# Layer 1 of a two-layer backbone: another order for its last two tiles, its weights' places and its mask's load

## The chip, the cores and the metric

One core of one Trainium2 chip runs the whole program. The time is that of one execution on the device in microseconds (us), the median of several runs. Beside it there is one execution taken by the hardware profiler, with its trace. Engines: PE is TensorE (matrix products and transposes), ACT is ScalarE, DVE is VectorE, POOL is GpSimd, SP is SyncE, which here only issues transfers. Each engine works through its instructions in order; a queue name with a q (SPq, POOLq) is an engine's sequencer when it issues a transfer.

## The reference

Two layers over 2048 latent tokens of width 1024 and 256 context tokens. Layer 0 (even) mixes latent attention and gated linear attention. Layer 1 (odd) is a neighbourhood attention over a grid of 32 by 64 tokens, with 16 heads of 64:

```python
q, k, v, z = jnp.split(h @ w_in, 4, axis=-1)          # 1024 columns each
q, k = rms_norm(heads(q), q_gain), rms_norm(heads(k), k_gain)
s = q . k (8 x 16 neighbours) * 64 ** -0.5 + bias     # and q . k_ctx * 64 ** -0.5
o = softmax(s) @ [v of the neighbours, v_ctx]
x = x + gate * ((o * silu(z)) @ w_out)
```

The products are kept in fp32 precision.

## The kernel before

**Products.** A matrix is split into a part hi that TensorE's fast fp32 format holds and the rest lo; a product is three matmuls, hi by hi (line 129), hi by lo (130) and lo by hi (131), over 8 slices of 128 rows: 24 matmuls of 128 x 512 for one cell. A cell is a tile t of 128 tokens (18 of them, 0 and 1 being context) by a group j of 512 columns of layer 1's weight `w_od`: j=0,1 are queries, 2,3 keys, 4,5 values, 6,7 the gate z.

**Weights.** Each j has 8 slices of 256 KB. A slice is loaded by SP into one of three buffers `wraw` (line 380), ACT copies it to the hi part (the helper at line 106), DVE subtracts for the lo part (line 383). The 32 KB a partition of one j, hi and lo, lies in one of four places, w0 to w3, and `OD_PLACE` says which. Places 0 and 1 belong to one pool, 2 and 3 to another. A generator, `od_steps`, makes the steps of one weight; `pump` takes a step at every fourth call while cells run, so that loads and splits are spread among them.

**Stages of layer 1.** `even_mix` ends layer 0 and loads j=2,3 ahead. `odd_qk` (line 1144) runs the cells of j=2,3,0,1 tile by tile, loads j=0,1 at the start and, each time the last cell of a j is done, loads one of the other four weights into the place that came free (`nxt`, `done`). Its last two tiles are written out by hand: all of j=0, then 1, 2, 3, and then j=6 on the same two tiles:

```python
cells += [(t, j) for j in (0, 1, 2, 3, 6) for t in (NT - 2, NT - 1)]
```

So from the second of these ten cells on, of some 5.5 us each, the 32 slices of the last four weights pass through `wraw`.

After a cell of `odd_qk` an activation squares it, DVE sums (`oss`) and scales it (`onat`, line 1182), and five steps into a later cell `fin` transposes it (`tp`, line 1190), scales it (`oqh`) and stores it: queries to `Q1` (hi and lo) and keys to `K1` from SP, keys besides as hi and lo in another layout, gathered over four tiles (`okt`), to `K1t` from POOL (`store_k`, line 1227, four stores of 512 KB for a block of four tiles). For j=6 the stores are z's, from POOL (line 1194).

`odd_vz` (line 1257) then runs j=7,4,5 for tiles 17 and 16, after that j=4 to 7 for the other tiles downwards, and at the very end j=4,5 alone for the context tiles 1 and 0. Woven in are the row maxima of the scores (`maxes`), which read back `K1` (`mk`), `Q1` (`mq`) and a table (`mtab`).

`odd_attention` (line 1356) works on eight pairs of heads. It loads the pair's keys of the context (`kc`), chunks of keys (`kt`), queries (`q`, hi and lo in `q10`, `q11` and `q20`, `q21`), values (`ov`) and two tables of biases (`tab0`, `tab1`, 517 KB each), all on SP and in the order written, since `load` chains them. POOL adds the mask `maskk` to both tables in place (line 1420). PE makes the scores (`st`, lines 1423 and 1424), DVE adds the table (`opt`, line 1587), ACT takes the exponential. For the first pair the loads are written ahead of the loop, the mask's last:

```python
Q[0, 1] = query(0, 1)
kt.append(chunk(0, 0))
V[0] = values(0)
tabs[0] = tables(0)
kc[0] = keys(0, 0, CTX, kcp, "kc")
Q[0, 0] = query(0, 0)
kt.append(chunk(0, 1))
values_ctx(0, V[0])
mk = self.tl(ap, [P, NR, NC], "maskk", bufs=1)
self.load(mk[:], self.i["maskk"].rearrange("p (r c) -> p r c", r=NR))
mask(tabs[0])
```

Buffers of the stages share the on-chip memory: a tile of a later stage lies where tiles of an earlier one were, and its load waits for their last reader. Waits and places follow from the pools; the order in which each engine gets its instructions is worked out when the program is built.

Of the kernel before, what the change touches and what calls it, by code (L numbers as in the profile page):

```python
# [10 lines left out]
F32 = mybir.dt.float32  # L11
F32R = mybir.dt.float32r
AF = mybir.ActivationFunctionType
ALU = mybir.AluOpType
# [3 lines left out]
P = 128  # L18
# [3 lines left out]
CTX = 256  # L22
# [66 lines left out]
class Kern:  # L89
# [919 lines left out]
    def even_mix(self, e1, win, hT):  # L1009
# [3 lines left out]
        with ExitStack() as es:  # L1013
# [57 lines left out]
            self.prep_pool(e1, "prp1", "left", 2, 3)  # L1071
            ws = [self.pool(e1, "owS", side="left", reuse_waits="tile")]

            def ahead():
                for j in (2, 3):
                    yield from self.od_steps(win, j, ws)
                for t in range(2):
                    hT[t] = self.prep(1, t, self.x1, pp, ("pj", 4))
                    yield
                    yield  # L1080
# [51 lines left out]
            next(ahead, None)  # L1132


    OD_PLACE = {2: 0, 3: 1, 0: 2, 1: 3, 4: 0, 5: 1, 6: 2, 7: 3}

    def od_steps(self, dst, j, ws):
        n = self.OD_PLACE[j]
        steps = self.split_steps(dst, j, ws[n // 2], self.i["w_od"][:, j], KD, 512, f"w{n}", 1)
        for k, _ in enumerate(steps):  # L1140
            if k % 2:
                yield

    def odd_qk(self, ws, win, hT):
        nc = self.nc
        self.V1c = self.scr("V1c", (2, P, NCT, 512), F32)
        self.V1 = self.scr("V1", (2, SEQ, 512), F32)
        self.Q1 = self.scr("Q1", (2, 8, P, SEQ), F32)
        self.z1 = self.scr("z1", (KD, P, SEQ), F32)
        self.K1 = self.scr("K1", (8, P, T), F32)  # L1150
        self.K1t = self.scr("K1t", (8, 2, P, T), F32)
        with ExitStack() as es:
            sp = self.pool(es, "osA", bufs=2, side="left", reuse_waits="tile")
            pp = self.pool(es, "opA", bufs=2, space=PSUM, reuse_waits="tile")
            qkg = self.tl(sp, [P, 2], "oqkg", bufs=1)
            nc.sync.dma_start(qkg[:], self.i["od_gain"])
            nc.vector.tensor_scalar(out=qkg[:, 0:1], in0=qkg[:, 0:1], scalar1=0.125, scalar2=None, op0=ALU.mult)
            self.ahead += [self.od_steps(win, 0, ws), self.od_steps(win, 1, ws)]
            pend, kt = [], {}

            def cell(t, j):
                hi, lo = hT[t]
                wh, wl = win[j]
                ps = self.tl(pp, [P, 8, 64], "gm", bufs=3)
                steps = self.mm3_steps(ps[:], (lambda k: hi[:, k, :], lambda k: lo[:, k, :]),
                                       (lambda k: wh[:, k, :], lambda k: wl[:, k, :]), range(KD))
                for n, _ in enumerate(steps):
                    if n == 5 and pend and (len(pend) > 1 or j == 6):
                        fin(*pend.pop(0))
                    yield  # L1170
                if j == 6:
                    n = self.tl(sp, [P, 512], "onat", bufs=4)
                    self.gate(n, ps[:].rearrange("p h d -> p (h d)"))
                    pend.append((t, j, n))
                    return
                sq = self.tl(sp, [P, 512], "osq")
                self.act(sq[:], ps[:].rearrange("p h d -> p (h d)"), AF.Square)
                ss = self.tl(sp, [P, 8], "oss", bufs=4)
                nc.vector.tensor_reduce(out=ss[:], in_=sq[:].rearrange("p (h d) -> p h d", h=8), axis=AX.X, op=ALU.add)
                self.rpow(ss[:], ss[:], 1.0 / 64, EPS)  # L1180
                n = self.tl(sp, [P, 512], "onat", bufs=4)
                nc.vector.tensor_tensor(out=n[:].rearrange("p (h d) -> p h d", h=8), in0=ps[:],
                                        in1=ss[:].unsqueeze(2).to_broadcast([P, 8, 64]), op=ALU.mult)
                pend.append((t, j, n))

            def fin(t, j, n):
                z = j // 2
                ps = self.tl(pp, [P, 4, P], "tp")
                for i in range(4):
                    nc.tensor.transpose(ps[:, i, :], n[:, i * P : i * P + P], self.ident[:])  # L1190
                hi = self.tl(sp, [P, 4, P], "oqh", F32R)
                if j == 6:
                    self.act(hi[:].bitcast(F32), ps[:])
                    nc.gpsimd.dma_start(self.z1[:4, :, (t - NCT) * P : (t - NCT) * P + P].rearrange("j p t -> p j t"), hi[:].bitcast(F32))
                    return
                self.act(hi[:], ps[:], AF.Copy, scale=qkg[:, z : z + 1])
                j0 = (j % 2) * 4
                if z == 1:
                    nc.sync.dma_start(self.K1[j0 : j0 + 4, :, t * P : t * P + P].rearrange("j p t -> p j t"), hi[:].bitcast(F32))
                if z == 0 or t < NCT:  # L1200
                    lo = self.tl(sp, [P, 4, P], "oql", F32R)
                    nc.vector.scalar_tensor_tensor(out=lo[:], in0=ps[:], scalar=qkg[:, z : z + 1], in1=hi[:],
                                                   op0=ALU.mult, op1=ALU.subtract)
                    if z == 0:
                        for part, tt in enumerate((hi, lo)):
                            nc.sync.dma_start(self.Q1[part][j0 : j0 + 4, :, (t - NCT) * P : (t - NCT) * P + P].rearrange("j p t -> p j t"),
                                              tt[:].bitcast(F32))
                    else:
                        store_k((hi, lo), j0, t * P, P)
                    return  # L1210
                g, r0 = divmod(2 * (t - NCT), 8)
                if r0 == 0:
                    kt[j] = [self.tl(sp, [P, 4, 512], f"okt{j}{part}", F32R, bufs=1) for part in range(2)]
                view = lambda x, n: x[:].rearrange("p i (r c b) -> p i r c b", r=n, c=4)
                for r in range(2):
                    oh, ol = (x[:].rearrange("p i (c b r) -> p i r c b", c=4, r=8)[:, :, r0 + r] for x in kt[j])
                    self.act(oh, view(ps, 2)[:, :, r], AF.Copy, scale=qkg[:, z : z + 1])
                    nc.vector.scalar_tensor_tensor(out=ol, in0=view(ps, 2)[:, :, r], scalar=qkg[:, z : z + 1],
                                                   in1=view(hi, 2)[:, :, r], op0=ALU.mult, op1=ALU.subtract)
                if r0 == 6:  # L1220
                    store_k(kt.pop(j), j0, CTX + g * 512, 512)

            def store_k(parts, j0, o, w):

                for u, x in enumerate(parts):
                    for i in range(2):
                        nc.gpsimd.dma_start(self.K1t[j0 : j0 + 4, i, u * 64 : u * 64 + 64, o : o + w].rearrange("j d t -> d j t"),
                                            x[i * 64 : i * 64 + 64].bitcast(F32))

            nxt = {2: 4, 3: 5, 0: 6, 1: 7}  # L1230
            done = lambda j: j in nxt and self.ahead.append(self.od_steps(win, nxt[j], ws))
            cells = self.cells(list(range(NT)), (2, 3, 0, 1), lambda t, j: j > 1 or t >= NCT)[:-8]
            cells += [(t, j) for j in (0, 1, 2, 3, 6) for t in (NT - 2, NT - 1)]
            for _ in self.stream(cells, hT, cell, lambda t: self.prep(1, t, self.x1, pp, ("px", 2)), done):
                self.pump()
            while pend:
                fin(*pend.pop(0))

    def gate(self, out, in_):

# [115 lines left out]
    def odd_attention(self, out, right, left, wout):  # L1356
# [4 lines left out]
        with ExitStack() as es:  # L1361
# [53 lines left out]
                    self.load(tb[:], self.i["rpb_k"][2 * j + i].rearrange("p (r c) -> p r c", r=NR))  # L1415
                return tabs

            def mask(tabs):
                for tb in tabs:
                    nc.gpsimd.tensor_tensor(out=tb[:], in0=tb[:], in1=mk[:], op=ALU.add)  # L1420

            def scores(ps, k1, k2, q1, q2):
                nc.tensor.matmul(ps, k1, q1, start=True, stop=False)  # L1423
# [87 lines left out]
            kt.append(chunk(0, 0))  # L1511
            V[0] = values(0)
            tabs[0] = tables(0)
            kc[0] = keys(0, 0, CTX, kcp, "kc")
            Q[0, 0] = query(0, 0)
            kt.append(chunk(0, 1))
            values_ctx(0, V[0])
            mk = self.tl(ap, [P, NR, NC], "maskk", bufs=1)
            self.load(mk[:], self.i["maskk"].rearrange("p (r c) -> p r c", r=NR))
            mask(tabs[0])  # L1520
            out_w, out_s = weights(), split()
            pend, late, OA = [], [], {}
            all_k, most_k = slice(0, KD), slice(0, KD - 1)
# [18 lines left out]
            for j in range(8):  # L1542
                OA[j] = {}, {}
                for s, (kind, n) in enumerate(steps):
                    g, c = divmod(n, 4)
                    if j < 7:
# [10 lines left out]
                            kc[j + 1] = keys(j + 1, 0, CTX, kcp, "kc")  # L1557
                        elif s == 10:
                            with self.tc.issue_after(self.psum.ins):
                                mask(tabs[j + 1])  # L1560
                    elif s % 2 and s < 16:
                        next(out_w)
                    pts = exps() if kind == "l" else [exps(), exps()]
# [197 lines left out]
```

## Time and profile before

| what | value |
|---|---|
| median of 3 runs | 3673.76 us (3667.17 to 3674.72) |
| profiled execution | 3676.2 us, span 3674.1 us |
| granted TensorE clock, mean | 0.982 |
| loads of `w_od` slices | 64 of 256 KB |
| key stores `K1t` | 32 of 512 KB, from POOL |

In the trace, times run from the start of the span. `odd_qk` starts at 2172 us, the ten cells of its last two tiles at 2547, `odd_vz` at 2623 (its first cell), the attention at 3088.9. A group reads: line, engine, operation, result<-operands. A wait reads: who waited at which line, for whom; total us, times, longest. A DMA's time in the chain runs from its issue to its landing. The clock column is the share of full TensorE speed that was granted, 0.5 being half speed.

### The profile page before, as it was taken

What the parts mean: (1) busy time and instruction counts of PE and PEld (TensorE: products, weight loads), DVE (VectorE), ACT (ScalarE), POOL (GpSimd) and SP (SyncE); (2) the same over time, 40 slices, a digit from 0 to 9 for tenths busy, and PEclk for the clock granted to TensorE, in tenths of its full rate; (3) what the DMA queues carried; (4) which work ended last, traced back from release to release, by engine and by line L of the source; (5) the groups of instructions that cost most, each with busy time, mean ns of one, the idle gap of its engine ahead of it and who ended that gap; (6) DMA issues with size and microseconds to landing.
All of it is one profiled execution on the core that took longest, in us unless ns stands there. A gap on an engine that the chain in (4) does not pass through costs nothing.

```text
span 3674.1 us, 51831 instructions
## 1 busy us (share of the span) xinstructions
PE 3565.7 (97%) x18404; PEld 2758.7 (75%) x18404; DVE 2363.0 (64%) x4860; ACT 1437.0 (39%) x2741; POOL 1205.6 (33%) x1336
## 2 busy tenths in 40 slices
PE   8999999999999999999999999999899999999998
PEld 6988998888886666655556878888688887555577
DVE  4677666888876666687664444454578784666721
ACT  5545551111125555555553124444422223555510
POOL 1433330101111212122201233333334443777743
PEclk9999999999999999999999999999999999999899
DMA  7455472222241232243622544455744447788554
GB/s 253 145 155 155 133 210 87 80 73 88 75 137 53 83 98 79 85 115 109 177 67 96 188 161 123 141 157 160 227 146 122 146 120 190 210 215 219 175 178 149
DMA packets 364372, 512.19 MB, mean 139 GB/s; under 512 B 25825, under 2 KB 243889, under 8 KB 358210
## 3 DMA queue, kind: packets, MB, share of 16 engines
q1 hardware_dynamic: 322642, 425.49, 39.8%
q0 software_dynamic: 19872, 55.92, 5.1%
q10 hardware_dynamic: 21600, 27.46, 2.1%
q8 instruction: 146, 2.39, 0.3%
q14 instruction: 112, 0.92, 0.1%
HBM read 329.38 MB, written 179.37 MB: 138 GB/s over the span
## 4 chain that ended last, share of the span: by engine, by line
PE 69%; issue 15%; POOL 5%; DVE 5%; DMA 4%; ACT 2%; SPq 0%; POOLq 0%; DVEq 0%; ACTq 0%
PE av L922 7%; PE gm L129 6%; PE gm L130 6%; PE gm L131 6%; PE st L980 4%; PE st L981 4%; PE st L982 4%; PE st L129 2%; PE st L131 2%; PE st L130 2%; PE pj L131 2%; PE pj L130 2%; PE pj L129 2%; PE o L1456 2%; DMA wraw<-w_od 1%
## 5 line engine op out<-in xcount | busy, mean ns | idle before, releaser
L971 DVE TENSOR_TENSOR acc<-acc,apt 128x512 f32<-128x512 f32 x512 | 364.8, 737 | 153.5 <-ACT apt L106 150.6
L106 ACT ACTIVATE apt<-st 128x512 f32<-128x512 f32 (+1 forms) x592 | 344.6, 594 | 290.5 <-PE st L982 257.4
L662 DVE TENSOR_REDUCE mm<-mx 128x1 f32<-128x512 f32 (+1 forms) x656 | 393.2, 630 | 89.9 <-PE mx L661 81.8
L922 PE MATMUL av<-apt,av 128*64 128x512 f32 (+1 forms) x1184 | 286.4, 599 | 0.0
L980 PE MATMUL st<-aq,akh 97*128 97x512 f32 (+1 forms) x592 | 255.7, 432 | 9.7 <-DMA aq<-QT 6.1
L661 PE MATMUL mx<-mk,mq 96*128 96x512 f32 (+1 forms) x656 | 238.6, 372 | 0.0
L981 PE MATMUL st<-aq,akh 96*128 96x512 f32 (+1 forms) x592 | 236.7, 400 | 0.0
L982 PE MATMUL st<-aq,akl 96*128 96x512 f32 (+1 forms) x592 | 235.3, 398 | 0.0
L1330 DVE CUSTOM_DVE_ANT_1 mx<-mx,mtab 128x217 f32<-128x217 f32 (+11 forms) x576 | 184.6, 338 | 49.2 <-PE mx L1324 37.9
L106 ACT ACTIVATE opt<-opt 128x930 f32<-128x930 f32 (+9 forms) x144 | 119.2, 830 | 248.0 <-POOL opt L1627 141.0
L106 ACT ACTIVATE u<-gm 128x352 f32<-128x352 f32 (+1 forms) x144 | 70.5, 496 | 360.4 <-PE gm L131 208.7
L1587 DVE TENSOR_TENSOR opt<-st,tab 128x64 f32<-128x64 f32 (+10 forms) x576 | 142.8, 316 | 88.2 <-PE st L1424 58.1
L922 PEld LDWEIGHTS av<-apt,av 128*64 128x64 f32 x1184 | 81.9, 138 | 156.4 <-issue 154.8
L980 PEld LDWEIGHTS st<-aq,akh 97*128 97x128 f32 x592 | 113.5, 192 | 101.6 <-issue 49.5
L1462 POOL TENSOR_TENSOR oacc<-oacc,opt 128x682 f32<-128x682 f32 (+10 forms) x144 | 169.8, 1199 | 26.4 <-ACT opt L106 25.1
L982 PEld LDWEIGHTS st<-aq,akl 96*128 96x128 f32 x592 | 114.6, 194 | 25.8
L661 PEld LDWEIGHTS mx<-mk,mq 96*128 96x128 f32 x656 | 122.7, 188 | 11.7
L981 PEld LDWEIGHTS st<-aq,akh 96*128 96x128 f32 x592 | 115.3, 195 | 18.3
L1423 PE MATMUL st<-q,kt 128*128 128x480 f32 (+5 forms) x256 | 99.6, 391 | 23.8 <-DVE opt L1587 18.9
L106 ACT ACTIVATE x<-px,modB,modA 128x128 f32<-128x128 f32 x272 | 99.3, 469 | 58.1 <-PE px L331 46.3
L129 PE MATMUL gm<-w0h,hhi 128*128 128x512 f32 x288 | 116.1, 403 | 0.0
L129 PE MATMUL gm<-w1h,hhi 128*128 128x512 f32 x288 | 115.7, 402 | 0.0
(570 smaller groups left out, 9928.1 us busy)
## 6 DMA issues: line engine op xcount, KB each, us to landing
q<-Q SPq DMA_DIRECT2D x48, 512.0 KB
H<-x ACTq DMA_DIRECT2D x36, 512.0 KB
adaw<-ada_w SPq DMA_DIRECT2D x64, 256.0 KB
x<-H SPq DMA_DIRECT2D x32, 512.0 KB
wraw<-w_od SPq DMA_DIRECT2D x64, 256.0 KB
K1t<-okt POOLq DMA_DIRECT2D x32, 512.0 KB, 7.6
kt<-K1t SPq DMA_DIRECT2D x32, 512.0 KB
mtab<-rpb_q SPq DMA_DIRECT2D x16, 899.0 KB
```

The lines of the kernel that those rows point to most:

```text
L106: return self.nc.scalar.activation(out, in_, func, **kw)
L129: self.nc.tensor.matmul(out, lh(k), rh(k), start=j == 0, stop=False)
L130: self.nc.tensor.matmul(out, lh(k), rl(k), start=False, stop=False)
L131: yield self.nc.tensor.matmul(out, ll(k), rh(k), start=False, stop=j == n - 1)
L661: mm = nc.tensor.matmul(ps[:, :w], q[:A_QK, (t % 6) * P : (t % 6) * P + P], k[:A_QK, k0 : k0 + w], start=True, stop=True)
L662: nc.vector.tensor_reduce(out=m[:, t, n : n + 1], in_=ps[:, :w], axis=AX.X, op=ALU.max)
L922: nc.tensor.matmul(O[j, nb][i * 64 : i * 64 + 64, :w], V[j, kt // TT][:, kt % TT, i * 64 : i * 64 + 64], pts[i][:, :w], start=n == 0, stop ...
L971: nc.vector.tensor_tensor(out=acc[i][:, :w], in0=a[:, :w], in1=pts[i][:, :w], op=ALU.add)
L980: nc.tensor.matmul(ps[:, :w], kh[: A_QK + 1, i, kq], qh[: A_QK + 1, :w], start=True, stop=False)
L981: nc.tensor.matmul(ps[:, :w], kh[:A_QK, i, kq], ql[:A_QK, :w], start=False, stop=False)
L982: mm = nc.tensor.matmul(ps[:, :w], kl[:A_QK, i, kq], qh[:A_QK, :w], start=False, stop=True)
L1330: nc.vector.tensor_tensor_reduce(out=s, in0=s, in1=tb[:, ri : ri + rn, ci : ci + cn], scale=1.0, scalar=-3e38, op0=ALU.add, op1=ALU.max, a ...
```

## The change

One generator now makes the steps for all weights in a list `todo`, two slices at a step, and splits the slices of the step before while it loads two new ones. `od_ahead` adds weights to the list:

```diff
-    OD_PLACE = {2: 0, 3: 1, 0: 2, 1: 3, 4: 0, 5: 1, 6: 2, 7: 3}
-
-    def od_steps(self, dst, j, ws):
-        n = self.OD_PLACE[j]
-        steps = self.split_steps(dst, j, ws[n // 2], self.i["w_od"][:, j], KD, 512, f"w{n}", 1)
-        for k, _ in enumerate(steps):
-            if k % 2:
-                yield
+    OD_PLACE = {2: 0, 3: 1, 0: 2, 1: 3, 6: 0, 7: 1, 4: 2, 5: 3}
+
+    def od_steps(self, dst, ws):
+
+        nc, todo, old, k = self.nc, self.todo, [], KD
+        while True:
+            new = []
+            for i in range(2):
+                if i < len(old):
+                    w, hi, lo = old[i]
+                    self.act(hi, w[:])
+                    nc.vector.tensor_tensor(out=lo, in0=w[:], in1=hi, op=ALU.subtract)
+                if k == KD and todo:
+                    j, k = todo.pop(0), 0
+                    n = self.OD_PLACE[j]
+                    dst[j] = [self.tl(ws[n // 2], [P, KD, 512], f"w{n}" + z, F32R, bufs=1) for z in "hl"]
+                if k < KD:
+                    w = self.tl(self.prp, [P, 512], "wraw", bufs=self.wbufs)
+                    nc.sync.dma_start(w[:], self.i["w_od"][:, j, k])
+                    new.append((w, *(x[:, k, :] for x in dst[j])))
+                    k += 1
+            old = new
+            if not (old or todo):
+                return
+            yield
+
+    def od_ahead(self, dst, ws, *js):
+
+        self.todo += js
+        if not self.ahead:
+            self.ahead.append(self.od_steps(dst, ws))
```

The key stores of a block are handed out one at a time, at every fourth step of a later cell; the last two tiles take j=2,3, then 0,1, then 6; the gate's weights 6 and 7 follow the keys and the values' 4 and 5 the queries, in other places than before:

```diff
+                    if n % 4 == 1 and out_k:
+                        out_k.pop(0)()
                     yield
...
                 if r0 == 6:
-                    store_k(kt.pop(j), j0, CTX + g * 512, 512)
+                    out_k.extend(store_k(kt.pop(j), j0, CTX + g * 512, 512))
...
-            nxt = {2: 4, 3: 5, 0: 6, 1: 7}
-            done = lambda j: j in nxt and self.ahead.append(self.od_steps(win, nxt[j], ws))
+            nxt = {2: 6, 3: 7, 0: 4, 1: 5}
+            done = lambda j: j in nxt and self.od_ahead(win, ws, nxt[j])
...
-            cells += [(t, j) for j in (0, 1, 2, 3, 6) for t in (NT - 2, NT - 1)]
+            cells += [(t, j) for j in (2, 3, 0, 1, 6) for t in (NT - 2, NT - 1)]
```

In the attention the first pair's tables take the mask from a copy of its own, loaded right behind them into a query buffer; the lasting copy is loaded where it was:

```diff
             tabs[0] = tables(0)
+            first = self.tl(qa, [P, SEQ], "q10", bufs=2)[:, : NR * NC]
+            mask(tabs[0], load_mask(first.rearrange("p (r c) -> p r c", r=NR)))
             kc[0] = keys(0, 0, CTX, kcp, "kc")
...
-            mk = self.tl(ap, [P, NR, NC], "maskk", bufs=1)
-            self.load(mk[:], self.i["maskk"].rearrange("p (r c) -> p r c", r=NR))
-            mask(tabs[0])
+            mk = load_mask(self.tl(ap, [P, NR, NC], "maskk", bufs=1)[:])
```

More of the change, by code (lines that the diff above doesn't have):

```diff
@@ L1072, in even_mix @@
             ws = [self.pool(e1, "owS", side="left", reuse_waits="tile")]
+            self.todo = [2, 3]
             def ahead():
-                for j in (2, 3):
-                    yield from self.od_steps(win, j, ws)
+                yield from self.od_steps(win, ws)
                 for t in range(2):
@@ L1157, in odd_qk @@
             nc.vector.tensor_scalar(out=qkg[:, 0:1], in0=qkg[:, 0:1], scalar1=0.125, scalar2=None, op0=ALU.mult)
-            self.ahead += [self.od_steps(win, 0, ws), self.od_steps(win, 1, ws)]
-            pend, kt = [], {}
+            self.od_ahead(win, ws, 0, 1)
+            pend, kt, out_k = [], {}, []
             def cell(t, j):
@@ L1208, in fin @@
                     else:
-                        store_k((hi, lo), j0, t * P, P)
+                        for f in store_k((hi, lo), j0, t * P, P):
+                            f()
                     return
@@ L1220, in fin, with store @@
                 if r0 == 6:
-                    store_k(kt.pop(j), j0, CTX + g * 512, 512)
+                    out_k.extend(store_k(kt.pop(j), j0, CTX + g * 512, 512))
             def store_k(parts, j0, o, w):
[L1225 to L1228, printed above, removed]
-            nxt = {2: 4, 3: 5, 0: 6, 1: 7}
-            done = lambda j: j in nxt and self.ahead.append(self.od_steps(win, nxt[j], ws))
+                def store(u, x, i):
+                    nc.gpsimd.dma_start(self.K1t[j0 : j0 + 4, i, u * 64 : u * 64 + 64, o : o + w].rearrange("j d t -> d j t"),
+                                        x[i * 64 : i * 64 + 64].bitcast(F32))
+                return [lambda u=u, x=x, i=i: store(u, x, i) for u, x in enumerate(parts) for i in range(2)]
+            nxt = {2: 6, 3: 7, 0: 4, 1: 5}
+            done = lambda j: j in nxt and self.od_ahead(win, ws, nxt[j])
             cells = self.cells(list(range(NT)), (2, 3, 0, 1), lambda t, j: j > 1 or t >= NCT)[:-8]
-            cells += [(t, j) for j in (0, 1, 2, 3, 6) for t in (NT - 2, NT - 1)]
+            cells += [(t, j) for j in (2, 3, 0, 1, 6) for t in (NT - 2, NT - 1)]
             for _ in self.stream(cells, hT, cell, lambda t: self.prep(1, t, self.x1, pp, ("px", 2)), done):
@@ L1237, in odd_qk @@
                 fin(*pend.pop(0))
+            for f in out_k:
+                f()
     def gate(self, out, in_):
@@ L1416, in tables, with mask, load_mask @@
                 return tabs
-            def mask(tabs):
+            def mask(tabs, mk):
                 for tb in tabs:
-                    nc.gpsimd.tensor_tensor(out=tb[:], in0=tb[:], in1=mk[:], op=ALU.add)
+                    nc.gpsimd.tensor_tensor(out=tb[:], in0=tb[:], in1=mk, op=ALU.add)
+            def load_mask(mk):
+                self.load(mk, self.i["maskk"].rearrange("p (r c) -> p r c", r=NR))
+                return mk
             def scores(ps, k1, k2, q1, q2):
@@ L1559, in odd_attention @@
                             with self.tc.issue_after(self.psum.ins):
-                                mask(tabs[j + 1])
+                                mask(tabs[j + 1], mk)
                     elif s % 2 and s < 16:
```

## The prediction

> **What bounds the kernel now.** I read the engines' shares first, then a table of windows over layer 1, then what TensorE (PE) waited for there, and last the chain that ended last.
>
> ```profile
> span 3674.1 us, 51831 instructions
> PE 3565.7 (97%) x18404; PEld 2758.7 (75%) x18404; DVE 2363.0 (64%) x4860; ACT 1437.0 (39%) x2741; POOL 1205.6 (33%) x1336
> ```
>
> PE is busy for 97% of the span, and the change takes no matmul away and adds none. So only PE's idle time and its time at a low clock can be won or lost. In the stretch that the change touches (windows; the columns are length, PE, PEld, DVE, ACT, POOL, then granted clock, DMA share, GB/s):
>
> ```profile
> 2570.00:2600.00 30.00, 30.00 (x142) 24.71 (x142) 20.71 (x33) 15.97 (x28) 10.94 (x11) 1.00 0.82 245
> 2600.00:2645.00 45.00, 31.16 (x124) 24.28 (x123) 17.73 (x31) 18.41 (x31) 12.26 (x14) 0.81 0.87 279
> ```
>
> The first row, the middle of the last two tiles, runs 142 matmuls in 30 us with no gap; the second, their end, only 124 in 45 us. At 4.73 per us, 124 need 26 us, so some 18 us are lost. What PE waited for between 2150 and 2700 (total, times, longest):
>
> ```profile
> PE tp L1190 <- DVE onat L1182: 8.4, 3, 6.7
> PE tp L1282 <- DVE ovz L1242: 3.1, 1, 3.1
> PE tp L1190 <- ACT oqh L106: 3.0, 1, 3.0
> PE px L331 <- DVE x L328: 2.9, 1, 2.9
> ```
>
> The last row stands at the start of the stage (2195 us); the others are the tail. Their 6.7 + 3.1 + 3.0, the 0.8 us of a short one, and two stretches at half clock make the 18 us. Behind them, by the chain of waits, stand transfers, not engines:
>
> ```profile
> 2605.32 2.80 DMA wraw<-w_od
> ...
> 2611.56 8.38 DMA wraw<-w_od
> ...
> 2626.11 10.73 DMA z<-oqh
> ```
>
> A 256 KB weight slice that takes 2.80 us at 2605 takes 8.38 us at 2611. In between POOL issues the first burst of key stores; a second one goes out just ahead of the gate's store (POOL's timeline):
>
> ```profile
> 2605.99 1.31 POOL L1227 DMA_DIRECT2D K1t<-okt  x2 [6.67 <-ACT okt L106]
> ...
> 2623.64 2.48 POOL L1227 DMA_DIRECT2D K1t<-okt  x4 [0.33 <-ACT okt L106]
> 2626.11 0.76 POOL L1194 DMA_DIRECT2D z<-oqh  x1
> ```
>
> DVE works in order. The split of the late slice (2614.88, after 4.15 us of idling) stands before the gate's normalising step, and with that the 6.7 us stall of PE ends:
>
> ```profile
> 2614.88 0.69 DVE L383 TENSOR_TENSOR w1l<-wraw,w1h 128x512 fp32r<-128x512 f32 x1 [4.15 <-ACT w1h L106]
> ```
>
> **The change part by part.** The order of the instructions on each engine, as the two programs are built, is the same up to the last two tiles, names apart; SP and POOL first differ at about 2570 us. The load-ahead written as one generator, and the key stores handed out singly, hence move nothing before that point: 0 us, and the 2.9 us wait at 2195 stays. Even the single stores still come out four in a row for a block of keys. No work has to hide these edits, since no instruction changes its place; if one did, the nearest price is that wait, 2.9 us either way.
>
> *The tail.* The transfers that meet there (count, KB, median us to landing):
>
> ```profile
> wraw<-w_od SPq DMA_DIRECT2D x29, 256.0 KB
> K1t<-okt POOLq DMA_DIRECT2D x8, 512.0 KB, 7.9
> ...
> Q<-oqh SPq DMA_DIRECT2D x4, 256.0 KB
> Q<-oql SPq DMA_DIRECT2D x4, 256.0 KB
> K<-oqh SPq DMA_DIRECT2D x4, 256.0 KB
> ...
> z<-oqh POOLq DMA_DIRECT2D x2, 256.0 KB, 9.0
> ...
> V<-ovz POOLq DMA_DIRECT2D x4, 128.0 KB, 2.4
> ```
>
> Bytes are not saved, only reordered. With keys first the two bursts (8 x 512 KB = 4.2 MB) go out with the fourth and the sixth cell, at about 2578 and 2593 instead of 2606 and 2624, in the middle of the 32 slices. In the built program 25 slices are split before the gate's second activation, against 29 now. Now, what has landed by then is 29 slices, half the key stores, and the Q and K stores: 7.6 + 2.1 + 3.1 = 12.8 MB in the 44 us from 2570 to 2614, 290 GB/s. Afterwards it is 25 slices, all key stores and the K stores, 6.6 + 4.2 + 1.0 = 11.8 MB: 41 us at that rate, 48 us at the 245 GB/s of the first row. So the gate is freed between 2610.7 and 2618.2; I take 2614.1, between the two, since the bursts sit where the 245 was measured with no burst in it. The gate's transposes and the next cell follow 3.5 us later when no late slice stands between them (a normalising step, an activation, a DVE step and three transpose groups of 0.4 to 0.7 us), so that cell starts at 2617.6. Now it starts at
>
> ```profile
> 2623.03 0.78 PE L129 MATMUL gm<-w3h,hhi 128*128 128x512 f32 x1
> ```
>
> which is a gain of 5.4 us (1.3 to 8.8). The gate's store has no burst ahead of it any more: instead of 10.73 us it takes some 3 us, near the 2.4 us of the V stores on the same queue. Then DVE's memsets do not hold up ovz, and the 3.1 us of PE go, with 1.6 us of the half clock after it. Against that, the loads of the maxima (keys, table, queries) stand behind the last slice on SP: I allow 1.3 us (0 to 3), about one slice's share of the stream. Tail: -(5.4 + 3.1 + 1.6 - 1.3) = **-8.8 us**, with ends of -2 and -14.
>
> By the Trainium skill ("Trainium Kernel Development and Optimization", Key Constraints) transfers issued from SP, ACT and POOL all run on the same 16 DMA engines and interleave. That speaks against this part, since bursts on POOL take from the slices on SP wherever they are put. The 8.38 us against 2.80 us agree with it; by it alone the tail would gain nothing, which is the first rival below.
>
> *The places of the weights.* This part is in the dictionary alone, and the change does not tell of it. Weights j=4 and 5 (the values) move from places 0 and 1 to places 2 and 3. The attention's first keys, tables and queries lie in the memory of places 2 and 3, as the built programs show. The last four cells of the values stage are tiles 1 and 0 with j=4 and 5. Today they use places 0 and 1, so the loads below go out 20 to 28 us before these cells end (SP's timeline; the last row is the mask, which waits for the last cell):
>
> ```profile
> 3060.54 1.08 SPq L111 DMA_DIRECT2D kt<-K1t  x2
> ...
> 3065.81 1.45 SPq L111 DMA_DIRECT2D tab<-rpb_k  x2
> ...
> 3068.43 2.60 SPq L111 DMA_DIRECT2D q<-Q  x3
> ...
> 3088.69 0.34 SPq L111 DMA_DIRECT2D maskk<-maskk  x1
> ```
>
> ```profile
> SPq L111 <- PE gm L131: 13.1, 3, 7.0
> ```
>
> That SP waits for matmuls of the projection here shows this reuse. Afterwards the first table has to wait for the low part of the very last cell, as the mask does now: 3088.69. SP is in order, so behind it queue the second table, the mask's copy, the first head's context keys and its queries, and PE's first score needs those queries. Sizes:
>
> ```profile
> q<-Q SPq DMA_DIRECT2D x6, 512.0 KB
> tab<-rpb_k SPq DMA_DIRECT2D x3, 517.0 KB
> ...
> maskk<-maskk SPq DMA_DIRECT2D x1, 517.0 KB
> ...
> kc<-K1t SPq DMA_DIRECT2D x1, 256.0 KB
> kc<-K1t SPq DMA_DIRECT2D x1, 128.0 KB
> ```
>
> 517 x 3 + 384 + 512 x 2 = 2959 KB. The first 517 KB take the time of the mask today,
>
> ```profile
> 3088.69 5.56 DMA maskk<-maskk
> ```
>
> and the other 2442 KB (2.50 MB) a rate that I take from windows around this place:
>
> ```profile
> 3070.00:3084.00 14.00, 14.00 (x65) 11.52 (x64) 0.00 (x0) 1.20 (x2) 1.18 (x2) 1.00 1.05 277
> ...
> 3088.00:3101.20 13.20, 8.96 (x36) 6.76 (x35) 7.90 (x20) 5.41 (x11) 5.37 (x4) 0.86 0.85 202
> 3101.20:3106.40 5.20, 5.20 (x18) 1.49 (x17) 1.20 (x9) 1.88 (x3) 4.96 (x4) 0.70 0.98 332
> ```
>
> The 277 GB/s hold for just these transfers: 9.0 us. The ends are 332 (7.5) and 216 of its slowest 4 us (11.6), the 202 being lowered by waits. So PE stalls 5.56 + 9.0 - 0.1 = 14.5 us (13.0 to 17.1). What stands there today goes,
>
> ```profile
> PE st L1423 <- DVE opt L1587: 4.2, 2, 3.6
> ```
>
> because the copy of the mask lands three transfers before the queries and POOL's two additions run meanwhile. The half clock that follows today, (1 - 0.86) x 13.2 + (1 - 0.70) x 5.2 = 3.4 us, stays, as a longer stall will not shorten it. All that waits behind the queries on SP (the next keys, the context values, the mask itself, the second head's queries) is late too; for that I add 1.5 us (0 to 4). Start of the attention: 14.5 - 4.2 + 1.5 = **+11.8 us** (8 to 17).
>
> By the Trainium skill ("DMA: Bandwidth & Descriptors", Where 436 GB/s comes from) a transfer between HBM and SBUF is bound by the HBM's share of one core, about 358 GB/s. By it the 2.50 MB would take 7.0 us and this part come to +9.8; no row here reaches that, so the sum goes by 277.
>
> *Sum:* -8.8 + 11.8 = +3.0 us. The profiled execution took 3676.2 us, 2.1 more than its span, so it would become 3679.2. It lies 2.4 us above the median of the runs; from 3673.76 I reach **3677 us**.
>
> **The rivals.** *The tail gains nothing* (slower): the bursts slow the slices in the middle as much as they do now at the end, the gate waits until 2618 or beyond, and the store of z and the loads of the maxima make a new wait. For it speaks the DMA share of 0.82 in the 30 us in which the bursts will come; against it, that today's slices wait only in the 8 us after a burst. Then -2 in the tail and +11.8 at the attention: 3684, up to 3689. It decides if a slice takes over 7 us at both bursts.
>
> *The loads are quick and the tail clears* (faster): of the 18 us all but 4 go, and the attention's loads run at 332 GB/s without a late effect: -14 + 8 = -6, 3668; with the half clock also cut, 3665. For it speaks that the tail's stalls all hang on transfers that move away; against it, that both ends must come together.
>
> *The mask alone* (faster): the attention's loads do not wait for the last cells, and the change does what its words say: 4.2 + 3.4 go at the attention and 8.8 in the tail, 3657. The reuse of places 2 and 3 speaks against it.
>
> **How the numbers follow.** Forecast 0.50, no gain in the tail 0.38, quick loads 0.09 (3662 to 3671), the mask alone 0.03. A measurement of this kernel can tell about 0.2% (7.3 us) from no change: faster is below 3666.4, slower above 3681.1. The forecast's own range, 3669 to 3685, lies mostly between; about a quarter of it is slower (0.12), and of the first rival some five sixths (0.32). Faster takes the mask alone (0.03), half of the quick loads (0.05) and the lowest end of the forecast (0.02). That gives 0.10 faster, 0.46 within, 0.44 slower. The range with 8 of 10 goes from 3667 to 3690: it leaves out the mask alone, half of the quick loads, and the worst end of the first rival.
>
> **What would show it.** Right: a gap of PE of 13 to 17 us before the first st of the attention, ended by a DMA of q; a wait of SP on gm just before the tables; no wait of st for opt of 3 us; the K1t stores in the tail some 28 us earlier; 7.5 us from the last product ahead of the gate's transposes to the next cell, where there are 12.9 now (to 2623.03), and no wait for ovz. Wrong: 11 us or more there, or the wait for ovz kept (the first rival), or table loads issued before the last cells end (the third), or a difference ahead of the last two tiles, which I hold to be nought.

## The result, and the profile after

| | before | after |
|---|---|---|
| median | 3673.76 us (3667.17 to 3675.64, 9 runs) | 3681.65 us (3677.87 to 3687.29, 9 runs) |
| ratio, 95% interval | | 1.0030 (1.0022 to 1.0039) |
| profiled execution, span | 3676.2, 3674.1 us | 3686.8, 3685.0 us |

The change makes the kernel slower, by 0.3% as the ratio has it (the two medians lie 7.9 us apart). The interval lies clear of no change. The time is 4.6 us above the predicted 3677, inside the range.

Four places of PE's timeline split the 10.9 us between the two spans: the first product of the stage of queries and keys (2172.03 us before, 2174.83 after), the end of the last product of the values stage (3088.89, 3090.52), the first score of the second pair of heads (3134.72, 3150.49), and the end of the span.

| stretch | before | after | difference |
|---|---|---|---|
| up to layer 1's first product | 2172.0 | 2174.8 | +2.8 |
| the two projection stages | 916.9 | 915.7 | -1.2 |
| attention, up to the second pair of heads | 45.8 | 60.0 | +14.1 |
| the rest of attention, and output | 539.4 | 534.5 | -4.9 |

The first row lies ahead of the first instruction that differs: two executions of one program differ by as much. The second and third are the prediction's two terms. In the last row the profile of before is the odd one: all other profiles of this document, of either order, have 532.2 to 537.0 us there.

The windows of the changed kernel's end of `odd_qk`, and of the attention's start (columns as before, the last three being clock, DMA share and GB/s):

```profile
2570.00:2600.00 30.00, 30.00 (x143) 24.75 (x142) 19.57 (x32) 19.04 (x34) 12.09 (x14) 1.00 0.71 219
2600.00:2645.00 45.00, 34.09 (x144) 27.07 (x142) 21.19 (x36) 17.11 (x30) 10.33 (x12) 0.85 0.88 270
...
3088.00:3118.00 30.00, 15.60 (x45) 11.35 (x46) 8.28 (x24) 6.81 (x12) 7.38 (x6) 0.63 0.95 241
```

In the last row PE works half of 30 us, at a granted clock of 0.63. For the first pair of heads, from its first score to the second pair's, the gap of PE left out, the clock was lower than before:

```profile
3104.52:3150.50 45.98, 44.87 (x261) 29.67 (x261) 23.42 (x71) 21.13 (x33) 27.80 (x23) 0.84 0.84 211
```

against 0.93 over the 45.8 us of before (3088.89 to 3134.71).

What PE waited for, at the tail (2150 to 2700 us), in the changed kernel:

```profile
PE tp L1216 <- DVE onat L1273: 8.2, 2, 6.8
PE px L331 <- DVE x L328: 4.5, 1, 4.5
PE tp L1216 <- DVE onat L1208: 2.2, 1, 2.2
...
PE mx L1348 <- ACT mz L106: 0.9, 1, 0.9
```

and at the attention's start (3060 to 3135 us):

```profile
PE st L1458 <- DMA q<-Q: 14.0, 1, 14.0
```

The wait for ovz (3.1 us) is gone, and so is the wait of the scores for the masked table (4.2 us). The wait for the gate is not: 8.2 us in place of 6.7 and 3.0. And one of 14.0 us stands where PE ran on before. SP's timeline of the changed kernel tells its cause:

```profile
3079.56 1.07 SPq L111 DMA_DIRECT2D kt<-K1t  x2
3080.86 0.41 SPq L111 DMA_DIRECT2D ov<-V  x1
3090.31 0.83 SPq L111 DMA_DIRECT2D tab<-rpb_k  x2
3091.19 0.42 SPq L111 DMA_DIRECT2D q<-maskk  x1
3091.71 1.01 SPq L111 DMA_DIRECT2D kc<-K1t  x2
3092.82 2.06 SPq L111 DMA_DIRECT2D q<-Q  x3
```

The tables, issued at 3065.81 before, go out at 3090.31, 0.2 us ahead of the end of the last projection product; mask, context keys and queries follow in line. The last of the queries that PE needs, in the chain of waits:

```profile
3093.46 10.93 DMA q<-Q
```

The bursts of key stores did move, some 23 to 25 us earlier (POOL's timeline, changed kernel). The store of z now has none close ahead of it:

```profile
2583.04 1.31 POOL L1254 DMA_DIRECT2D K1t<-okt  x2
2585.31 1.24 POOL L1254 DMA_DIRECT2D K1t<-okt  x2 [0.96 <-DVE onat L1208]
...
2598.81 1.30 POOL L1254 DMA_DIRECT2D K1t<-okt  x2 [9.46 <-ACT okt L106]
...
2600.50 1.25 POOL L1254 DMA_DIRECT2D K1t<-okt  x2
...
2626.91 0.83 POOL L1220 DMA_DIRECT2D z<-oqh  x1 [15.27 <-ACT oqh L106]
```

but the slice issued behind each burst is as late as the one of before was (8.38 us), against 2.5 us for a slice on its own (chain of waits, changed kernel):

```profile
2586.38 8.71 DMA wraw<-w_od
...
2604.51 10.67 DMA wraw<-w_od
...
2622.72 2.48 DMA wraw<-w_od
```

### The profile page after: what moved, and what is told of

Read it like the earlier page. It is cut to its first block, busy times and chain, and to the rows that moved or that the text cites. A ratio compares the mean times of both kernels' runs of the same rounds, so it can differ in the third digit from the quotient of the medians.

```text
span 3685.0 us, 51822 instructions
## 1 busy us (share of the span) xinstructions
PE 3565.4 (97%) x18404; PEld 2758.8 (75%) x18404; DVE 2363.8 (64%) x4860; ACT 1438.1 (39%) x2741; POOL 1206.1 (33%) x1336
## 4 chain that ended last, share of the span: by engine, by line
PE 68%; issue 15%; DVE 5%; DMA 5%; POOL 4%; ACT 3%; SPq 0%; POOLq 0%; DVEq 0%; ACTq 0%
PE av L922 7%; PE gm L129 6%; PE gm L131 6%; PE gm L130 6%; PE st L980 4%; PE st L981 3%; PE st L982 3%; PE o L1491 2%; PE st L129 2%; PE st L131 2%; PE st L130 2%; PE st L1458 2%; PE pj L131 2%; PE pj L130 2%; PE pj L129 2%
## 5 line engine op out<-in xcount | busy, mean ns | idle before, releaser
L1497 POOL TENSOR_TENSOR oacc<-oacc,opt 128x682 f32<-128x682 f32 (+9 forms) x144 | 169.6, 1202 | 18.7 <-ACT opt L106 17.3
L202 POOL TENSOR_TENSOR oss<-oss,mhalf 128x8 f32<-128x8 f32 x68 | 112.8, 1659 | 5.1
```

## The experiments

### The places of the values' weights

First, the context tiles moved in the values stage, so that the last four cells read places 0 and 1:

```diff
             cells = [(t, j) for j in (7, 4, 5) for t in (NT - 1, NT - 2)]
-            cells += self.cells(list(range(NT))[::-1], (4, 5, 6, 7), lambda t, j: j < 6 or t >= NCT)[8:]
+            cells += [(t, j) for j in (4, 5) for t in (1, 0)]
+            cells += self.cells(list(range(NCT, NT))[::-1], (4, 5, 6, 7))[8:]
```

> The changed kernel, and in the values stage the context tiles 1 and 0 go right after tiles 17 and 16, so that the last four cells are those of the gate (j=6,7) in places 0 and 1, and places 2 and 3 fall free four cells (some 22 us) earlier. Theory (the attention's first loads wait for the last reader of places 2 and 3): the 14.0 us gap ahead of the first score falls under 1 us and with it the half clock behind it (some 3 to 4 us); about 3682 - 17 = 3665 us. Rival (the mask's copy, 517 KB more ahead of the queries on SP, makes the stall): a gap of 10 us or more stays and the time stays within 5 us of 3682.

Measured: 3683.86 us, ratio to before 1.0025 (1.0014 to 1.0036). The wait for q is gone: the tables go out at 3061.88. But the time is not better, as another wait stands there (PE's waits at the attention's start, and the chain behind them):

```profile
PE tp L1313 <- ACT ozt L106: 12.9, 2, 10.3
```

```profile
3087.53 10.20 DMA z<-ozt
...
3098.45 2.16 DMA z<-ozt
```

The last four cells are now the gate's. Each puts its transposed result into the one buffer `ozt` and stores it. One such store of 256 KB queues behind the attention's loads and takes 10.20 us; the next, when these are through, 2.16. So the theory's place was right and its price went elsewhere. Next, therefore, the same with the gate written back into its own tile, which leaves four tiles to take turns:

```diff
-                n = self.tl(sp, [P, 512], "ovz", bufs=3)
+                n = self.tl(sp, [P, 512], "ovz", bufs=4)
...
-                z = self.tl(sp, [P, 4, P], "ozt", bufs=1)
-                self.act(z[:], pt[:])
+                z = n[:].rearrange("p (i t) -> p i t", i=4)
+                self.act(z, pt[:])
```

> The changed kernel with the context tiles early in the values stage, and the transposed gate written back into its own tile, of which there are four, in place of one separate buffer. Theory (with the context early, what was left was PE waiting 10.3 us for that one buffer, whose store queued behind the attention's loads): no wait over 2 us between the last cells and the scores, and as the tail of the odd_qk stage is some 3 us shorter, 3665 to 3670 us, faster than both. Rival (the transfers at that place are too many in any order): a wait of 8 us or more turns up at another buffer or at the first scores, 3678 to 3684 us.

Measured: 3669.06 us, ratio to before 0.9991 (0.9982 to 1.0000). Left at that place are these waits:

```profile
PE st L1459 <- DVE opt L1623: 2.3, 4, 1.1
PE tp L1313 <- ACT ovz L106: 2.2, 1, 2.2
```

The second is slightly over the 2 us expected. The stall is gone with its cause. "Faster than both" is not clear of noise against the kernel of before, as the interval ends at 1.0000. As a control, the gate in place alone, on the changed kernel:

> The changed kernel with the transposed gate written back into its own tile alone, the context tiles last. Theory (the places of the values' weights make the stall): the gap of 13 to 15 us ahead of the first score stays, 3679 to 3683 us. Rival (the one buffer of the transposed gate slowed the whole stage): the time falls by more than 5 us with the gap still there.

Measured: 3682.24 us (ratio to before 1.0023, 1.0014 to 1.0031), with

```profile
PE st L1458 <- DMA q<-Q: 13.8, 1, 13.8
```

So the 13 us between these last two kernels are the place of the last cells' weights, not the buffer. The stretch from the last projection product to the second pair of heads says the same: 46.5 us with the context early, 58.7 without.

### The mask's copy

The changed kernel without the copy (the mask loaded last, as before):

> The changed kernel without the mask's copy: the mask is loaded last, as before. Theory (places): 517 KB less stand ahead of the queries, so PE waits some 12 us for q instead of 14.0, and then 2 to 5 us for the masked table, whose load now stands behind queries and keys; 3681 to 3685 us. Rival (the copy makes the stall): no gap over 3 us ahead of the first score, the old one of 4.2 us at the table, 3671 to 3674 us.

Measured: 3684.03 us, ratio to before 1.0029 (1.0019 to 1.0038).

```profile
PE st L1454 <- DMA q<-Q: 12.4, 1, 12.4
PE st L1454 <- DVE opt L1618: 1.7, 2, 1.1
```

The stall is there without the copy. With 517 KB (0.53 MB) less ahead of the queries it is 1.6 us shorter: 331 GB/s for what is added to such a queue, by two single executions. The table's wait of 1.7 us is below the 2 to 5 expected; the scores on context keys cover most of it. And the other way round, the copy alone on the kernel of before:

> The kernel of before with the mask's copy alone. Theory (the places decide, and in the old places the copy lands early): the 4.2 us that the scores wait for the masked table go, and the half clock behind them (3.4 us), with no wait for queries in their place; about 3674 - 7 = 3667 us. Rival (the copy delays the queries): PE waits for q at the first score by 2 us or more, and the time is 3674 or above.

Measured: 3672.72 us, ratio 0.9993 (0.9985 to 1.0002). The same stretch (3080 to 3130 us) with the copy and, for comparison, in the next kernel, which has the program of before:

```profile
PE st L1427 <- DVE opt L1591: 2.1, 3, 1.1
```

```profile
PE st L1454 <- DVE opt L1618: 3.4, 2, 2.3
```

The copy shortens the wait, with no wait for queries in its place; so the rival misses too. But it is worth 1 to 2 us, not 7: in that execution of the old order the wait is 3.4 instead of 4.2, and 2.1 of it stay with the copy. From the last projection product to the second pair of heads it takes 42.7 us, against 45.1 to 45.8 in three profiles of the old order without the copy; then the second pair takes 47.4 us instead of 46.0, so about half is given back. A gain of 7 us is outside the interval, 2 inside. What it is worth in the time is not resolved here.

### The load-ahead and the single stores

> The load-ahead as one generator and the key stores handed out singly, with the old order of the last two tiles, the old places and the old mask. Each engine has the same instructions in the same order as before. Theory: no difference, 3674 us within 2 us, and the wait at 2195 us between 2.5 and 4.5 us as executions differ. Rival (these two parts cost the 1 to 2 us by which that wait was longer after): 3676 us, the wait at 4.5.

Measured: 3672.85 us (3663.28 to 3679.0), ratio 0.9993 (0.9983 to 1.0003); the wait at 2195 us was 2.6. The two parts do nothing that these runs can tell, as expected; the 4.5 us of the changed kernel's profile is a matter of one execution (2.3 to 3.3 in five other profiles of that order).

### The tail

The eight key stores of the last block held back on POOL, behind the second store of z (`zstore`), on the changed kernel:

```diff
-                    if n % 4 == 1 and out_k:
+                    if n % 4 == 1 and out_k and t < NT - 2:
...
+            with self.tc.issue_after(self.zstore.ins):
                 for f in out_k:
                     f()
```

> The changed kernel with the eight key stores of the last block held back on POOL behind the second store of z, so that no burst runs beside the 32 weight slices. Theory (bytes decide: ahead of the slice that frees the gate stand 25 slices, the key and the query stores and both bursts, 13.9 MB, of which 4.2 go): the slices land in 3 us each, and from the last product ahead of the gate's transposes to the next cell it takes 3 us or less instead of 9.6. The loads of the maxima lie in the memory of the held stores and come later: a wait of mx of 8 to 12 us takes its place, the time 3680 to 3687 us. Rival (the order of DVE and ACT decides, not the transfers): the 9.6 us stay within 2.

Measured: 3689.25 us, ratio to before 1.0048 (1.0034 to 1.0062). PE's timeline at the gate, changed kernel and then this one (the last product ahead of it, the two groups of transposes, the next cell):

```profile
2617.96 0.40 PE L131 MATMUL gm<-w0h,hlo 128*128 128x512 f32 x1
2619.74 0.66 PE L1216 MATMUL tp<-ident,onat 128*128 128x128 f32 x4 [1.39 <-DVE onat L1273]
2627.19 1.12 PE L1216 MATMUL tp<-ident,onat 128*128 128x128 f32 x4 [6.79 <-DVE onat L1273]
2627.95 0.78 PE L129 MATMUL gm<-w1h,hhi 128*128 128x512 f32 x1
```

```profile
2611.60 0.40 PE L131 MATMUL gm<-w0h,hlo 128*128 128x512 f32 x1
2615.29 0.66 PE L1216 MATMUL tp<-ident,onat 128*128 128x128 f32 x4 [3.29 <-DVE onat L1274]
2620.12 1.12 PE L1216 MATMUL tp<-ident,onat 128*128 128x128 f32 x4 [4.18 <-DVE onat L1274]
2620.89 0.78 PE L129 MATMUL gm<-w1h,hhi 128*128 128x512 f32 x1
```

From the start of the stage the next cell comes 5.1 us sooner (2620.89 - 2172.88 = 448.0 against 453.1; 1.4 of it is the wait at 2195 us, 3.1 against 4.5). Against four other profiles of the changed order (452.2 to 453.4) it is 4.1 to 5.4. That is the price of the bursts. But the gap ahead of it is 8.9 us, not 3: with the stores gone, the slices still hold the gate. The theory was half right. The time is above the 3680 to 3687 expected, and the new wait came at another place: not at the maxima, but PE waits 12.0 us for ovz, since a memset on DVE ahead of it waits for the held stores:

```profile
2628.73 15.87 DMA K1t<-okt
...
2644.74 0.21 DVE L1337 MEMSET mm<- 128x80 f32 x2 [16.97 <-DMA K1t<-okt]
```

Without bursts the slices in the chain of waits land in 2.6 to 4.8 us, and yet 29 of them take this long to issue (first and last start in us, of the held-back kernel):

```profile
L1154 SPq DMA_DIRECT2D wraw<-w_od x29: 327/328/677, 2569.5 to 2613.4; - x29
```

43.9 us by 28 is 1.57 us a slice, or 167 GB/s. All transfers together move 216 GB/s from 2570 to 2614 us, below what the DMA engines do a little later in this trace (340 at 2630 to 2640). A load waits until one of three buffers is free, and ACT until the load has landed. This gives a second theory: the turn of the three buffers sets the pace. Its test is a fourth buffer in the kernel of before (`osq` gives up a buffer, and the gate is written in place, for room):

```diff
-            self.prep_pool(e1, "prp1", "left", 2, 3)
+            self.prep_pool(e1, "prp1", "left", 2, 4)
...
-                sq = self.tl(sp, [P, 512], "osq")
+                sq = self.tl(sp, [P, 512], "osq", bufs=1)
```

> The kernel of before, with four buffers wraw, one buffer for the squares, and the transposed gate written back into its own tile (three of them). Theory (the three buffers' turn holds the old tail too): the 12.9 us from the last product ahead of the gate's transposes to the next cell fall to 7 or less; 3664 to 3669 us. Rival (only the bursts hold it there, as they come with the last slices): 11 us or more, 3671 to 3675 us.

Measured: 3660.28 us, ratio to before 0.9964 (0.9952 to 0.9976).

```profile
L380 SPq DMA_DIRECT2D wraw<-w_od x28: 327/328/460, 2562.5 to 2596.9; - x28
```

34.4 us by 27 is 1.27 us a slice; the last goes out at 2596.9 instead of 2618.7. The next cell starts 442.5 us into the stage, 8.5 earlier than before, and the time is below the range expected. The gap itself was 8.3 us (12.9 before), between the two expectations, because the products ahead of it end sooner too. Of the 8.5 us, 2.1 come from the start of the stage, where the same buffers turn: the wait of 2.9 us there fell to 0.8. What the single buffer for the squares does was not tried alone; the gate in place alone brought nothing on the changed kernel (3682.24 against 3681.65). So the gain is put down to the fourth buffer by what the slices did, not by a run with it alone. Both together, held stores and four buffers:

> The changed kernel with the key stores held back behind the gate's and with four buffers wraw (squares and gate as in the other two). Theory (three buffers' turn and bursts together hold the gate): with neither, 4 us or less from the last product ahead of the gate's transposes to the next cell, where there were 9.6 with both and 8.9 without the bursts; the 12 us wait for the held stores stays, so some 3680 to 3686 us. Rival (the order of DVE and ACT decides): 7 us or more.

Measured in one run: 3673.79 us, below the range expected. The last product ahead of the gate ends at 2601.6, the next cell starts at 2604.56, 437.1 us into the stage:

```profile
2602.29 0.66 PE L1216 MATMUL tp<-ident,onat 128*128 128x128 f32 x4 [0.69 <-DVE onat L1274]
2604.15 0.66 PE L1216 MATMUL tp<-ident,onat 128*128 128x128 f32 x4 [1.20 <-DVE onat L1274]
2604.56 0.50 PE L129 MATMUL gm<-w1h,hhi 128*128 128x512 f32 x1
```

3.0 us: with neither bursts nor the three buffers the gate hardly waits. The order of ACT and DVE alone does not hold it. The held stores still cost a wait for ovz, of 11.4 us.

### Versions that beat both

Four buffers on the kernel with the context early:

> As the kernel with the context early and the transposed gate in place (3669 us), with four buffers wraw for the weight slices in place of three; the room comes from one buffer for the squares instead of two, and three tiles for gate and values instead of four. Theory (what is left at the gate, 8.9 us even without bursts, is the turn of three buffers: 4.2 us from a load to the end of its split, 1.4 us a slice): 1.05 to 1.2 us a slice, the 32 slices done some 8 us earlier, the 9 us ahead of the next cell down to 5 or less; 3662 to 3666 us. Rival (the transfers' rate is the limit): the slices land later each, the 9 us stay within 2, 3667 to 3671 us.

Measured: 3660.89 us, ratio to before 0.9969 (0.9958 to 0.9981). The next cell starts 1.8 us after the last product ahead of the gate, but a slice that is late beside the bursts still holds PE for 4.5 us before that:

```profile
PE tp L1216 <- DVE onat L1208: 4.5, 1, 4.5
```

The time is below the range expected, but the pace of 1.05 to 1.2 us a slice was missed by far. Here is that pace in six profiles, one for each case, from the start of ACT's first copy of the 32 slices to that of its last, by 31:

| us a slice | three buffers | four buffers |
|---|---|---|
| old order, bursts near the end | 1.81 | 1.39 |
| changed order, bursts in the middle | 2.07 | 1.78 (context early) |
| changed order, bursts held back | 1.59 | 1.36 |

In the changed order the bursts cost some 0.4 to 0.5 us a slice and the want of a fourth buffer 0.2 to 0.3: both hold the stream, and the bursts more. The best of these is near the pace at which the program hands the slices out: `pump` gives four to a cell of some 5.5 us, 1.4 us a slice. Whether that is the limit that is left was not tested.

And the mask's copy on the kernel of before with four buffers:

> The kernel of before with four slice buffers (3660.28 us) and the mask's copy besides. Theory (the copy takes away the wait for the masked table, 3.9 us there, at no price in the old places): that wait falls to 2 us or less in two pieces, 3657 to 3660 us. Rival (given back in the heads behind it, as with the copy alone): the wait goes, but the time stays within 2 us of 3660.

Measured: 3658.24 us, ratio to before 0.9968 (0.9957 to 0.9979). The wait for the table falls from 5.6 us in all to 2.9 (in five pieces; 2 or less in two were expected), and the time agrees with both expectations. Of the versions run it has the lowest median, but it can't be told from the one without the copy.

## Why the prediction was right and where it was wrong

**The attention's start: right in mechanism, one part of its sum wrong.** The step said that the first table has to wait for the last cell's low weights, 14.5 us of stall (13.0 to 17.1); it was 14.0, ended by q, with SP's issue of the tables moved to 3090.31. It vanished when the last cells read other places, and stayed without the copy. For the whole start +11.8 us were forecast (8 to 17). Measured up to the second pair of heads it is +14.1 (45.8 to 60.0), and other executions agree: 45.1 to 45.8 in three profiles of the old order without the copy, 58.7 to 60.1 in five with the stall. What was too small is the half clock behind the gap. The prediction let it stay at 3.4 us, "as a longer stall will not shorten it"; it did not shorten, it grew. After the 3.6 us gap of before the clock was 0.5 for some 6.7 us, after the 14.0 us gap for some 15 us, which loses 7.5 us, 4.1 more. With that, 14.0 - 4.2 + 4.1 = 13.9 is nearly all of the 14.1, and the 1.5 us set down for loads that come late are hardly there.

The Trainium skill ("DMA: Bandwidth & Descriptors", Where 436 GB/s comes from) gives about 358 GB/s as the HBM's limit for a core; an estimate with it makes the stall 12.4 us. The trace has 14.0, nearer to the 14.5 by the measured 277 GB/s; the added copy by itself went at 331. That "no row here reaches" 358 holds for the rows shown, but not for every stretch: before, 361 GB/s were moved from 3068 to 3072 us.

**The tail: the step that failed.** "25 slices, all key stores and the K stores, 6.6 + 4.2 + 1.0 = 11.8 MB", at 245 to 290 GB/s, and from that a gain of 5.4 us at the gate. Three things were wrong in it. First, the stores of the queries were left out. With queries computed after the keys, their hi and lo (2.1 MB) stand in the same stretch, so that the sum is the 13.9 MB that the experiment with the held stores starts from, no less than the 12.8 of before. Second, the 290 GB/s are not in the trace: by a window from 2570 to 2614 us the DMA engines moved 241, so that not all of the 12.8 MB fell there. Third, the sum has no term for the three buffers, which hold the slices at 1.59 us each even without bursts (1.36 with four buffers), nor for what a burst in the middle adds (2.07). The cell behind the gate started 453.1 us into the stage, against 451.0 before (and 452.7 and 453.0 in two other profiles of the old order): no gain, as the first rival had it ("the tail gains nothing": 3684 us, measured 3681.65). That rival was to be decided by slices of over 7 us at both bursts; they took 8.71 and 10.67, and 4 to 5 us were won at the gate when the bursts were held back. The sign named for the gap ahead of that cell came out between the two: 9.6 us, where 7.5 was to show the forecast right and 11 wrong. The gap is shorter than the 12.9 of before because the products ahead of it end later (443.5 us into the stage instead of 438.1).

By the Trainium skill ("Trainium Kernel Development and Optimization", Key Constraints) transfers from SP, ACT and POOL share the 16 DMA engines. The traces agree at two places: the slice of 10.67 us against 2.48, and the store on ACT's queue of 10.20 us against 2.16.

**The store of z: right.** The wait for ovz (3.1 us) went when no burst stood ahead of the store, and one of 12.0 us, for the held stores themselves, came when they were put behind it. The new wait for the maxima was 0.9 us, forecast 1.3. This is what is left of the tail's gain: 1.2 us over the two stages, below the lower end of 2 that was given.

**The load-ahead and single stores: right.** Their program is the same in order, and the time was too.

**The mask's wait: right that it goes, too large in what it brings.** The 4.2 us were one execution's, and in the old order 2.1 us of waiting for the table's sums stay when the mask is early.

**The weights.** "Within 0.2%" had 0.46 and "slower" 0.44; it was slower by 0.3%, since the term of gain was mis-sized by 7.6 us (-8.8 forecast, -1.2 measured) and the term of loss by only 2.3. That the time still lies in the range 3667 to 3690 is no proof of the forecast: the range held its first rival too. And that 3677 is missed by so little is partly luck, as the two errors add up to 9.9 us and executions of one program differ by more than that.

## What to carry to other kernels

When weights or tiles change their places, look up which tiles of the *next* stage lie in the same memory, and which reader is the last one there: a dictionary entry moved 3 MB of loads from under 22 us of products to behind them. Before transfers are reordered to relieve a stream of loads, add up all transfers of the stretch, compare with what the trace's windows show as moved there, and look how often a load waits for a free buffer. Here the bursts of stores and the number of buffers both held the stream, and the kernel of before with one more buffer gained 0.36%, more than any order that was run with three. And price a gap of PE together with the half clock behind it, which here grew with the gap.

## What was not expected of the hardware

Another queue did not get round a full one: a store of 256 KB on ACT's queue took 10.20 us while the mask and the queries of the next heads were under way on SP's queue, and 2.16 us after. The half clock lasted some 15 us after a gap of 14.0 us, though PE was busy for nearly all of it, against some 6.7 us after one of 3.6. In the four other profiles with that stall it cost 5.5 to 7.4 us within 46 us of the first score. And one program differs from run to run by more than the effects looked for: the kernel with the load-ahead and the single stores alone, which has the order of before, took 3663.28 to 3679.0 us in 12 runs. In its profile one pair of heads takes 46.0 us and the next 47.4.
